# A hybrid decoder layer on one core: the order of the weight loads in the ten-set phase, and the tile of the fourth input sum

## The chip, the cores and the metric

The kernel runs on one core of one Trainium2 chip. The core has a matrix engine (PE), a vector engine (DVE), a scalar engine (ACT), a general-purpose engine (POOL) and a synchronisation engine (SP). SP, ACT and POOL can issue DMA transfers between the chip's memory (HBM) and the core's on-chip memory; the profile shows the issues of SP in queue q1 and those of POOL in queue q0. The metric is the device time of one execution in microseconds; the time of a kernel is the median of its runs.

## What is computed

One layer of a decoder trunk for 256 tokens of width 2048: an RMSNorm, one wide input projection, two token mixers side by side (gated linear attention and differential attention), two branch projections, a gated merge, an output projection, a second RMSNorm and the residual. Cut to what matters here:

```python
h = rmsnorm(x, pre_norm_g[l])
proj = h @ w_in[l]
(a_q, a_k, a_v, a_g, a_lr, b_q, b_k, b_v, b_g, m_a, m_b) = jnp.split(proj, offsets, axis=-1)
gk = jax.nn.log_sigmoid(a_lr @ gla_gk_w2[l] + gla_gk_b[l]) / GATE_LOGIT_NORMALIZER
o_a = rmsnorm(gla_chunked(a_q, a_k, a_v, gk), gla_norm_g[l]) * jax.nn.silu(a_g)
o_b = rmsnorm(diff_attention(b_q, b_k, b_v, lam), diff_norm_g[l]) * (1.0 - lam_init)
o_b = o_b * jax.nn.silu(b_g)
merged = jax.nn.sigmoid(m_a) * (o_a @ w_branch_a[l]) + jax.nn.sigmoid(m_b) * (o_b @ w_branch_b[l])
x = x + rmsnorm(merged @ w_out[l], post_norm_g[l])
```

The weights and the inputs are float32. The change touches the stage that computes ten blocks of 1024 columns of `proj` (a_g, b_v, b_g, m_a and m_b).

## The kernel before

**Halves.** All weights pass through PE in pieces of 128 x 1024 values, called halves, in one fixed sequence (`seq`). For each half ACT rounds it to a high part (`hi`, line 355), DVE subtracts to get the low part (`lo`, line 356), and PE multiplies with both (line 563): six matmuls of 512 columns for a half of a set. `take` hands PE the next half; it calls `emit_half` so that three halves (`AHEAD`) are written into the program ahead of the one in use. `hi` and `lo` have three buffers each.

**Sets.** The ten sets are computed with seven products in place of eight block products (Strassen's way): the 2048 rows and the 1024 columns are cut into two by two blocks, and `PRODUCTS = (1, 3, 2, 5, 6, 7, 4)` is the order in which `block_products` takes them. Each product has two tiles (t = 0, 1) of two halves (h = 0, 1), so a set has 28 halves. Their weights are:

- `a`, two tiles of 128 x 2048: the first row block. It is the operand of product 1. Then the second block is added to it in memory by DMA, and later DVE adds to it on the chip, so that products 5, 6 and 4 read changed values.
- `b`, two tiles: the fourth block. It is the operand of product 3; during products 5 and 6 DVE adds `b` to `a`, then the second block is added to `b` by DMA, and product 7 reads it.
- `c`, four tiles of 128 x 1024: the third block, the operand of product 2, added to `a` during product 7.

The first load of `a` or `b` is a "link" (`link`, line 223: 1 MB, from SP for set 0, from POOL for the others), and the additions by DMA are line 248 (0.5 MB each, POOL). `a` and `b` come from a pool of six tiles, tag `chain`. `c` comes from the pool `big`, tag `u`, which has 18 tiles for everything of this size: the split input `xs` (eight tiles through the whole phase), the raw input `xraw` (four), gate halves `gr` and `gl`, parts of q and k, and more. `c` is loaded by SP (line 240).

**Partners.** Between the halves of a set stand halves of other matrices (`v4`, `k..`, `q..`, then `dq..`, `dk..`), two in a tile called `raw` with three buffers (line 306, SP). A set of the steady part has three such tiles, their halves behind products 2, 5, 6 and 7; set 0 has four more halves.

**Order.** The framework orders the instructions of each engine itself, by their place in the program and by when their inputs and tiles are ready in its own model. `tc.keep_in_program_order` pins an instruction behind the one of the same engine that stands before it in the program. In the set phase the matmuls, the links, the additions by DMA and the spills are pinned. The loads of `c` and of `raw` are not, so a load may go out ahead of one that stands before it in the program. All DMAs of POOL stand in one line, and an instruction that waits holds up those behind it; the same goes for SP.

**Where the links and spills stand.** Before, the links of the next set are written at products 6 (`a`) and 7 and 4 (`b`). The gate halves `gr` and `gl` of a set are spilled to memory by POOL at `SPILL_AT` in the next set, that is at product 5; a `u` tile is free when its spill has landed.

**Input sums.** Products 3, 5, 6 and 7 multiply with sums of input blocks (`s4`, `r1`, `s2`, `r3`), made by `sum_operands` before the phase, but for the fourth, `r3`: `last_sum` (lines 741 to 745) is written into the phase after six steps (`PUT_OFF`) and takes a `u` tile of its own. The other three are made in two tiles of the `chain` pool, `temps`; each has two halves, and the second half of `temps[1]` is not used:

```python
r1, s2, s4 = (temps[n // 2][:, n % 2] for n in range(3))
```

`last_sum` is the last reader of `xraw[0]` and `xraw[1]`.

**The loads in `emit_half`.** A raw tile's load is written into the program when its first half is the next to be emitted:

```python
while loaded[0] < min(j + 2, len(seq)):
    if len(seq[loaded[0]]) == 3 and seq[loaded[0]][2] == 0:
        load(loaded[0])
    loaded[0] += 1
```

Of the kernel before, what the change touches and what calls it, by code (L numbers as in the profile page):

```python
# [14 lines left out]
P = 128  # L15
# [15 lines left out]
MERGE = (0, 1, 6, 7)  # L31
GLA_GATES = (8, 9)
LEAD = 11
PAIRS = [(g, pair) for g in range(4) for pair in range(2)]
EARLY = 3
PARTNERED = ((2, 1), (5, 1), (6, 0), (6, 1), (7, 0), (7, 1))
MORE_PARTNERS = ((0, 1, 0), (0, 1, 1), (0, 3, 1), (0, 5, 0))
SPILL_AT = (5, 0, 0)
PACE = {"linear": 1.5, "pairs": 1.75}
BIG = 18  # L40
MORE = 16
# [58 lines left out]
def phase_steps():  # L100

    keys = ["v4"] + [f"{name}{hf}{c}" for hf in range(2) for name in ("k", "q") for c in range(4)]
    keys += [f"{name}{g}{c}" for g, pair in PAIRS[:EARLY] for name in ("dq", "dk") for c in (2 * pair, 2 * pair + 1)]
    other = [(key, r, h) for key in keys for r in range(4 if key == "v4" else 1) for h in range(2)]
    slots = [(s, prod, t) for s in range(SETS) for prod in PRODUCTS for t in range(2)]
    mixed = []
    for slot in slots:
        mixed += [("set", *slot, h) for h in range(2)]
        s, prod, t = slot
        for _ in range(((prod, t) in PARTNERED) + (slot in MORE_PARTNERS)):  # L110
            mixed.append(other.pop(0))
    return mixed + other
# [11 lines left out]
def branch_steps():  # L124

    plain = [("y03", r, h) for r in (2, 3) for h in range(2)]
    plain += [(f"y1{g}", r, h) for g in range(2) for r in range(2) for h in range(2)]
    parts = half_set_steps("ys0")
    return [(plain, parts)[n == "p"].pop(0) for n in BRANCH_ORDER]


def late_steps():

    plain = [(f"y1{g}", r, h) for g in (2, 3) for r in range(4) for h in range(2)]
    plain += [(f"o{g}", r, h) for r in range(2) for g in range(2) for h in range(2)]
    parts = half_set_steps("os0") + half_set_steps("os1")
    return [(plain, parts)[n == "p"].pop(0) for n in LATE_ORDER]
# [3 lines left out]
def hybrid_kernel(ctx: ExitStack, tc, xt, xn, preg, postg, w, w2, gkb, glag, lamv, diffg, ident_d, causal_d, lmask_d, out):  # L141
    nc = tc.nc
    pe, act, dve, pool, sp = nc.tensor, nc.scalar, nc.vector, nc.gpsimd, nc.sync
# [12 lines left out]
    def u(shape, name, dtype=F32):  # L156
        count[0] += 1
        return big.tile(shape, dtype, tag="u", name=f"{name}_{count[0]}")
# [28 lines left out]
    def f32(ap):  # L187
        return ap.bitcast(F32)
# [10 lines left out]
    def halves_of(*keys):  # L199
        return [(key, r, h) for key in keys for r in range(len(at[key])) for h in range(2)]  # L200

    def heads_order(pairs):
        return halves_of(*(f"{name}{g}{c}" for g, pair in pairs for name in ("dq", "dk") for c in (2 * pair, 2 * pair + 1)))

    seq = halves_of("v0", "v2", "v3") + phase_steps()
    seq += heads_order(PAIRS[EARLY:]) + halves_of(*(f"y0{g}" for g in range(4)))[:-4]
    seq += branch_steps() + late_steps() + halves_of("o2", "o3")
    ready = {}
    emitted = [0]
    raws = {}  # L210
    chain = {}

    def weights(key, r):
        a, size = at[key][r]
        return w[a : a + P * size].rearrange("(p n) -> p n", p=P), size

    def block(s, i, t):
        return weights(f"set{s}", 2 * i + t)[0]
# [8 lines left out]

    def emit_set(s, prod, t, h):
        c = slice(1024 * h, 1024 * h + 1024)
        name, i = {(6, 0): ("a", 0), (6, 1): ("a", 1), (7, 1): ("b", 0), (4, 0): ("b", 1)}.get((prod, t), (None, 0))  # L230
        if h == 0 and name and s + 1 < SETS:
            link(s + 1, name, i)
        if h == 0 and s == 0 and prod == 1:
            link(s, "b", t)
        for ahead in range(min(2, SETS - s)):
            n = 4 * (PRODUCTS.index(prod) - PRODUCTS.index(2)) + 2 * t + h - 28 * ahead + (LEAD if s + ahead else 6)
            if 0 <= n < 4:
                i, j = n // 2, n % 2
                raws[s + ahead, i, j] = u([P, 1024], "c")
                sp.dma_start(raws[s + ahead, i, j], block(s + ahead, 2, i)[:, 1024 * j : 1024 * j + 1024])  # L240
        a, b = chain[s, "a", t], chain[s, "b", t]
        return raws[s, t, h] if prod == 2 else (b if prod in (3, 7) else a)[:, c]

# [50 lines left out]
    def load(j):  # L294
        key, r, h = seq[j]
        src, size = weights(key, r)
        n = size // 2
        early = key == "v0"
        if key == "v3" and r == 0:
            for i in range(2):  # L300
                link(0, "a", i)
        count[0] += 1
        raw = raws[key, r] = wpool.tile([P, 2048], F32, tag="raw", name=f"raw_{count[0]}")
        cuts = (0, n, size) if j in (0, 2) else (0, size)
        for a, b in zip(cuts, cuts[1:]):
            i = sp.dma_start(raw[:, a:b], src[:, a:b])
            if early or key[0] == "o" or key in ("y10", "y11", "y12", "y13", "ys0"):
                tc.keep_in_program_order(i)
        if early and j // 2 in X_LOADS:
            load_x(*X_LOADS[j // 2])  # L310

    def emit_plain(j, key, r, h):
        n = at[key][r][1] // 2
        if key == "v0":
            if j:
                prep_x(j)
            if 6 <= j < 14:
                square_x(j - 6)
        return raws[key, r][:, n * h : n * h + n]

    loaded = [0]

    def emit_half():
        j = emitted[0]
# [77 lines left out]
    def square_x(i):  # L402
        src = xraw[i // 2][:, 2 * (i % 2) : 2 * (i % 2) + 2, :].rearrange("p a t -> p (a t)")
        t = t2([P, 512], "xsq") if i else ssum
        tc.keep_in_program_order(act.activation(t, src, AF.Square))
        if i:
            dve.tensor_tensor(out=ssum, in0=ssum, in1=t, op=ALU.add)
# [96 lines left out]
    done = set()  # L504
# [55 lines left out]
    pinned = [False]  # L560
# [144 lines left out]
    def sum_operands():  # L705
        for kt in range(KT):
            x = xraw[kt // 4][:, kt % 4, :]
            act.activation(x, x, AF.Copy, scale=preg_s[:, kt : kt + 1])
            if kt % 4 == 3:
                yield  # L710
        temps = []
        for n in range(2):
            count[0] += 1
            temps.append(blocks.tile([P, 2, 8, P], F32, tag="chain", name=f"temp_{count[0]}", bufs=6))
        r1, s2, s4 = (temps[n // 2][:, n % 2] for n in range(3))

        def part(i, j, q):
            return xraw[2 * j + q][:, :, P * i : P * i + P]

        def rows(t, q):  # L720
            return t[:, 4 * q : 4 * q + 4]

        def split(name, t):
            hi, lo = (blocks.tile([P, 8, P], F32R, tag=f"{name}{e}", name=f"{name}{e}", bufs=1) for e in "hl")
            act.activation(hi, t, AF.Copy)
            dve.tensor_tensor(out=lo, in0=t, in1=f32(hi), op=ALU.subtract)
            sums[name] = hi, lo

        for q in range(2):
            dve.tensor_tensor(out=rows(r1, q), in0=part(1, 1, q), in1=part(1, 0, q), op=ALU.subtract)  # L730
            dve.scalar_tensor_tensor(out=rows(s2, q), in0=rows(r1, q), scalar=-1.0, in1=part(0, 0, q), op0=ALU.mult, op1=ALU.subtract)
        yield
        for q in range(2):
            dve.scalar_tensor_tensor(out=rows(s4, q), in0=rows(s2, q), scalar=-1.0, in1=part(0, 1, q), op0=ALU.mult, op1=ALU.subtract)
        split("s4", s4)
        yield
        split("r1", r1)
        yield
        split("s2", s2)

        def last_sum():
            r3 = u([P, 8, P], "r3")
            for q in range(2):
                dve.tensor_tensor(out=rows(r3, q), in0=part(0, 0, q), in1=part(1, 0, q), op=ALU.subtract)
            split("r3", r3)

        put_off.append(last_sum)

    def late():
# [32 lines left out]
    def others():  # L782
# [7 lines left out]
        for hf in range(2):  # L790
            for name in ("k", "q"):
                part = u([P, 2, 4, P], name)
                for c in range(4):
                    o = ps("bg")
                    for h in range(2):
# [10 lines left out]
                        yield  # L806
        for g, pair in PAIRS[:EARLY]:
            for name in ("dq", "dk"):
# [24 lines left out]
    def block_products(s):  # L833
# [20 lines left out]
        for prod in PRODUCTS:  # L854
# [3 lines left out]
            for t in range(2):  # L858
                for h in range(2):
                    if (prod, t, h) == SPILL_AT:  # L860
                        settle_owed()
# [41 lines left out]

    sets = (step for s in range(SETS) for step in block_products(s))
    rest = others()
    pinned[0] = True
    fetched = []
    for n, step in enumerate(phase_steps()):
        if n == PUT_OFF:
# [3 lines left out]
        next(sets if step[0] == "set" else rest)  # L913
    for gen in (sets, rest):
        assert next(gen, DONE) is DONE
    pinned[0] = False
    joint.close()
    more = ctx.enter_context(tc.tile_pool(name="more", bufs=MORE))
    pools[:] = ctx.enter_context(tc.tile_pool(name="small", bufs=2)), more
# [377 lines left out]
    m0 = gspill[12:16]  # L1297
    for g, pair in PAIRS[EARLY:]:
        diff_heads(g, pair)
# [251 lines left out]
    for g in (2, 3):  # L1551
# [7 lines left out]
        if g == 2:  # L1559
            total(0, 2, bank, 2)  # L1560
            for b in range(2):
                xres.append([])
                for i in range(2):
                    t = u([P, 1024], "xres")
# [3 lines left out]
    t = total(0, 3, bank)  # L1568
# [10 lines left out]
    for c in range(2):  # L1579
# [6 lines left out]
        if c == 0:  # L1586
            t = cell(1, 3)[:, :256]
# [4 lines left out]
        else:  # L1592
            end = ps("bg")
            c = slice(TURNED[0] % 1024, TURNED[0] % 1024 + 512)
            t = yg[1, 1][:, c]
# [67 lines left out]
```

## Time and profile before

| | |
|---|---|
| median of 3 runs | 1094.99 us (1094.82 to 1095.22) |
| the profiled execution | 1098.81 us |
| its span, first to last instruction | 1097.0 us |
| mean granted TensorE clock | 0.993 |
| matmuls | 5380 |
| DVE, ACT busy | 88%, 69% of the span |
| moved by DMA | 295.55 MB, mean 269 GB/s |
| DMA queues, share of 16 engines | q1 (SP) 42.8%, q0 (POOL) 42.3% |

The profile shows one execution. Busy time of PE overstates its work, since matmuls overlap and their ends are modelled; where PE waits is better read from the starts of its matmuls in the chain of work that ended last. A row of the timeline gives start, length, engine, line, operation, output<-inputs, and in brackets the idle time of the engine just before it and what ended it. Tiles go by their names in the program without numbers: `mm` and `bg` are accumulation banks, `in_w_dram` the packed weights. "DMA to landing" counts from the issuing instruction's start to the arrival of the last byte. The phase of the ten sets runs from about 84 to 652 us of the span.

### The profile page before, as it was taken

The page shows a single profiled execution, that of the slowest core. Times are in us where ns is not written, and L with a number is a line of the kernel's source. Part 1 is how long each engine was busy: PE and PEld are TensorE (multiplying, and loading weights), DVE is VectorE, ACT ScalarE, POOL GpSimd, SP SyncE. Part 2 cuts the span into 40 slices and gives each one's busy share as a digit, 9 for nine tenths or more (in the row PEclk, how much of TensorE's full clock was granted, in tenths as well). Part 3 has the DMA queues.
Part 4 walks back from the last instruction along what each step waited for, and adds up shares of the span by engine and source line. Part 5 has one row for each costly group of instructions (what it writes and reads, how often), then busy time and mean ns, then how long its engine had stood idle before and what let it go on. Part 6 is the DMA issues. An engine that isn't in the chain of part 4 may idle for free.

```text
span 1097.0 us, 15424 instructions
## 1 busy us (share of the span) xinstructions
PE 1075.8 (98%) x5380; PEld 917.7 (84%) x5380; DVE 963.6 (88%) x1289; ACT 758.1 (69%) x1090; POOL 177.3 (16%) x259
## 2 busy tenths in 40 slices
PE   9999899999999999999999999999999999999997
PEld 8998788888878888878788888898987888888886
DVE  7887989999999999989899998985877878889896
ACT  7886676777676767667676776665766777566662
POOL 0211212121212121221121212013110112100000
PEclk9999999999999999999999999999999999999999
DMA  9898987989797979797979778759988998989752
GB/s 354 284 324 242 291 254 209 343 215 327 208 338 205 353 205 351 200 329 191 350 167 373 173 250 307 230 201 333 310 299 257 282 312 266 338 292 259 268 187 101
DMA packets 68366, 295.55 MB, mean 269 GB/s; under 512 B 8832, under 2 KB 11904, under 8 KB 51648
## 3 DMA queue, kind: packets, MB, share of 16 engines
q1 hardware_dynamic: 38080, 167.99, 42.8%
q0 software_dynamic: 29632, 125.84, 42.3%
q8 instruction: 42, 0.69, 0.3%
q10 hardware_dynamic: 576, 0.73, 0.2%
q14 instruction: 36, 0.29, 0.1%
HBM read 267.27 MB, written 27.26 MB: 268 GB/s over the span
## 4 chain that ended last, share of the span: by engine, by line
PE 82%; DVE 6%; DMA 5%; issue 4%; ACT 2%; POOL 1%; POOLq 0%; ACTq 0%; DVEq 0%
PE mm L563 56%; PE bg L563 17%; DMA b<-in_w_dram 3%; DVE lo L356 2%; PE mm L551 2%; PE bg L551 2%; PE mm L536 1%; PE bg L997 1%; DMA dh<-dh 1%; PE bg L536 1%; DVE a L256 1%; ACT hi L355 1%; ACT prob L1142 1%; DMA c<-in_w_dram 1%; DVE prob L1136 1%
## 5 line engine op out<-in xcount | busy, mean ns | idle before, releaser
L355 ACT ACTIVATE hi<-raw 128x1024 fp32r<-128x1024 f32 (+3 forms) x213 | 217.7, 1026 | 122.5 <-PE mm L563 68.1
L356 DVE TENSOR_TENSOR lo<-raw,hi 128x1024 fp32r<-128x1024 f32 (+3 forms) x215 | 252.6, 1180 | 34.0 <-ACT hi L355 31.8
L355 ACT ACTIVATE hi<-a 128x1024 fp32r<-128x1024 f32 x160 | 168.8, 1060 | 47.8 <-PE mm L563 30.9
L356 DVE TENSOR_TENSOR lo<-a,hi 128x1024 fp32r<-128x1024 f32 x160 | 190.1, 1219 | 6.1 <-ACT hi L355 4.6
L563 PE MATMUL mm<-hi,xs 128*128 128x512 f32 (+1 forms) x608 | 155.9, 382 | 1.4 <-ACT hi L355 1.4
L563 PEld LDWEIGHTS mm<-hi,xs 128*128 128x128 f32 x608 | 113.9, 188 | 20.4 <-ACT hi L355 1.8
L563 PE MATMUL bg<-xs,hi 128*128 128x512 f32 x448 | 117.8, 396 | 0.0
L355 ACT ACTIVATE hi<-b 128x1024 fp32r<-128x1024 f32 x80 | 84.6, 1060 | 40.2 <-DMA b<-in_w_dram 19.1
L356 DVE TENSOR_TENSOR lo<-b,hi 128x1024 fp32r<-128x1024 f32 x80 | 97.9, 1223 | 15.6 <-ACT hi L355 13.0
L563 PEld LDWEIGHTS bg<-xs,hi 128*128 128x128 f32 x448 | 86.2, 192 | 17.3
L563 PE MATMUL mm<-lo,xs 128*128 128x512 f32 (+1 forms) x304 | 88.6, 381 | 0.1
L563 PE MATMUL mm<-xs,hi 128*128 128x512 f32 x320 | 82.2, 394 | 0.0
L248 POOL DMA_DIRECT2D b<-in_w_dram x40 | 35.0, 875 | 210.1 <-DVE a L256 78.4
L563 PEld LDWEIGHTS bg<-xs,lo 128*128 128x128 f32 x448 | 60.9, 190 | 6.3 <-DVE lo L356 2.1
L563 PEld LDWEIGHTS mm<-xs,hi 128*128 128x128 f32 x320 | 57.4, 189 | 10.0
L563 PEld LDWEIGHTS mm<-lo,xs 128*128 128x128 f32 x304 | 56.8, 188 | 10.1 <-DVE lo L356 0.5
L563 PE MATMUL bg<-xs,lo 128*128 128x256 f32 x448 | 62.9, 283 | 0.7 <-DVE lo L356 0.7
L356 DVE TENSOR_TENSOR lo<-c,hi 128x1024 fp32r<-128x1024 f32 x40 | 49.0, 1226 | 9.1 <-ACT hi L355 5.0
L355 ACT ACTIVATE hi<-c 128x1024 fp32r<-128x1024 f32 x40 | 42.5, 1063 | 15.3 <-PE mm L563 10.5
L563 PE MATMUL mm<-hi,oah 128*128 128x512 f32 x128 | 50.6, 396 | 0.5 <-DVE part L1309 0.5
L563 PE MATMUL mm<-hi,oal 128*128 128x512 f32 x128 | 50.1, 391 | 0.0
L256 DVE TENSOR_TENSOR a<-a,b 128x1024 f32<-128x1024 f32 x40 | 48.9, 1222 | 0.7
(407 smaller groups left out, 2280.5 us busy)
## 6 DMA issues: line engine op xcount, KB each, us to landing
raw<-in_w_dram SPq DMA_DIRECT2D x90, 1024.0 KB, 7.9
c<-in_w_dram SPq DMA_DIRECT2D x40, 512.0 KB, 12.4
a<-in_w_dram POOLq DMA_DIRECT2D x40, 512.0 KB, 9.6
b<-in_w_dram POOLq DMA_DIRECT2D x40, 512.0 KB, 10.0
a<-in_w_dram POOLq DMA_DIRECT2D x18, 1024.0 KB, 14.6
b<-in_w_dram POOLq DMA_DIRECT2D x18, 1024.0 KB, 9.9
raw<-in_w_dram SPq DMA_DIRECT2D x14, 832.0 KB, 6.8
gr<-gr POOLq DMA_DIRECT2D x10, 512.0 KB, 6.2
```

The source lines that it names most:

```text
L248: tc.keep_in_program_order(pool.dma_start(chain[s, name, i][:, c], block(s, 1, i)[:, c], accum_op=ALU.add))
L256: add = dve.tensor_tensor(out=a, in0=a, in1=chain[s, "b", i][:, c] if second else raws[s, i, h], op=ALU.add)
L355: act.activation(hi_t[:, a:b], r[:, a:b], AF.Copy)
L356: dve.tensor_tensor(out=lo_t[:, a:b], in0=r[:, a:b], in1=f32(hi_t[:, a:b]), op=ALU.subtract)
L536: i = pe.matmul(out, lhs, rhs, start=first and n == 0, stop=last and n == len(pairs) - 1, **kw)
L551: i = pe.matmul(banks[g][b][:, :n], a[part][:, P * b : P * b + P], w[:, n * g : n * g + n], start=first, stop=last)
L563: i = pe.matmul(*args, **kw)
L997: pe.matmul(o, xk[:, P * c : P * c + P], xq.rearrange("p (b c t) -> p b c t", b=2, c=4)[:, :, c, :], start=i == 0, stop=i == 1)
L1136: dve.tensor_tensor_reduce(out=prob[m][:, lo:up], in0=banks[b][:, n * m : n * m + n], in1=cm[:, lo:up], scale=1.0, scalar=-3e38, op0=ALU.a ...
L1142: act.activation(prob[m][:, lo:up], prob[m][:, lo:up], AF.Exp, scale=score_scale[:, b : b + 1], bias=mx[:, i : i + 1], accum_out=z[:, i : ...
```

## The change

Four things are changed, and no arithmetic. First, the links of `a` for the next set are written at product 3 (second tile) and product 2 (first tile) in place of product 6; those of `b` stay. Second, the gate halves of the set before are spilled at product 3 in place of product 5. Third, within the phase the loads of `c` and of `raw` are pinned to program order, and at three places of each set (`RAWS_AT`) the next raw tile that isn't loaded yet is loaded early, as long as fewer than three are in use by the program's count (`alive`). Fourth, `r3` is computed in the unused half of `temps[1]`.

```diff
+LINKS = {(3, 1): ("a", 0), (2, 0): ("a", 1), (7, 1): ("b", 0), (4, 0): ("b", 1)}
+RAWS_AT = ((4, 1, 0), (2, 0, 1), (5, 1, 0))
-SPILL_AT = (5, 0, 0)
+SPILL_AT = (3, 0, 0)
...
     def emit_set(s, prod, t, h):
-        name, i = {(6, 0): ("a", 0), (6, 1): ("a", 1), (7, 1): ("b", 0), (4, 0): ("b", 1)}.get((prod, t), (None, 0))
+        name, i = LINKS.get((prod, t), (None, 0))
...
-                sp.dma_start(raws[s + ahead, i, j], block(s + ahead, 2, i)[:, 1024 * j : 1024 * j + 1024])
+                tc.keep_in_program_order(sp.dma_start(raws[s + ahead, i, j], block(s + ahead, 2, i)[:, 1024 * j : 1024 * j + 1024]))
+        if (prod, t, h) in RAWS_AT:
+            load_next(emitted[0])
...
     def load(j):
+        alive[0] += 1
-            if early or key[0] == "o" or key in ("y10", "y11", "y12", "y13", "ys0"):
+            if early or joint_loads[0] or key[0] == "o" or key in ("y10", "y11", "y12", "y13", "ys0"):
                 tc.keep_in_program_order(i)
...
     def emit_plain(j, key, r, h):
+        alive[0] -= h
...
+    def load_next(done):
+        j = max(loaded[0], done)
+        while j < len(seq) and not (len(seq[j]) == 3 and seq[j][2] == 0):
+            j += 1
+        if j < len(seq) and alive[0] < 3:
+            load(j)
+            loaded[0] = j + 1
...
         def last_sum():
-            r3 = u([P, 8, P], "r3")
+            r3 = temps[1][:, 1]
...
-    pinned[0] = True
+    pinned[0] = joint_loads[0] = True
...
-    pinned[0] = False
+    pinned[0] = joint_loads[0] = False
```

Written out for a set of the steady part, the program order of SP's loads becomes: the first two `c` of the next set, its first raw tile, the other two `c`, and then, within the next set, its second and third raw tile. In set 0 it is: four `c`, then the raw tiles of `v4` one after another.

More of the change, by code (lines that the diff above doesn't have):

```diff
@@ L318, in emit_plain @@
                 square_x(j - 6)
+        alive[0] -= h
         return raws[key, r][:, n * h : n * h + n]
     loaded = [0]
+    joint_loads = [False]
+    alive = [0]
+    def load_next(done):
[5 more added lines that the diff above has]
+            loaded[0] = j + 1
     def emit_half():
```

## The prediction

> **What bounds the kernel now.** I read the page's busy times first.
>
> ```profile
> PE 1075.8 (98%) x5380; PEld 917.7 (84%) x5380; DVE 963.6 (88%) x1289; ACT 758.1 (69%) x1090; POOL 177.3 (16%) x259
> ```
>
> PE carries the time, and the change leaves its matmuls alone. What can be won is PE's idle time between 84 us and 652 us, where the ten sets run. The chain in order of time gives it: columns are start, length, what.
>
> ```profile
> 84.47 2.18 PE bg L563 x12
> ...
> 144.18 2.77 PE bg L563 x16
> 146.95 21.78 PE mm L563 x96
> ...
> 201.79 21.78 PE mm L563 x96
> ...
> 651.71 26.71 PE mm L563 x144
> ```
>
> A row of 96 matmuls (16 halves: the last product of one set and the first three of the next) starts each period. 201.79 - 146.95 = 54.84 us is a period without a wait. Nine of them would take 493.6; from 146.95 to 651.71 there are 504.8. **Sets 1 to 9 lose 11.2 us.** The stretch from 84.47 to 146.95 holds 22 halves of set 0 (at 21.78/16 = 1.36), eight of `v4` (2.18) and two of `k00` (2.77): 52.9 us of work in 62.5, so **set 0 loses 9.6**. Together 20.8 us, which is all that this change can win.
>
> Next, windows (us, PE, PEld, DVE, ACT and POOL busy, granted clock, DMA share, GB/s) around the worst places, and the waits between 147 and 652 us (total, times, longest).
>
> ```profile
> 276.60:281.00 4.40, 4.40 (x24) 3.74 (x23) 4.23 (x4) 3.24 (x4) 0.06 (x1) 1.00 0.01 2
> 281.00:306.60 25.60, 25.60 (x131) 21.83 (x130) 24.62 (x25) 14.91 (x17) 6.77 (x10) 1.00 0.97 286
> 259.00:276.60 17.60, 17.60 (x79) 14.60 (x78) 16.24 (x16) 14.84 (x16) 3.50 (x4) 1.00 0.96 243
> ...
> 132.00:139.00 7.00, 6.41 (x15) 4.85 (x16) 7.00 (x8) 4.46 (x5) 1.08 (x2) 0.52 1.00 370
> 473.00:482.00 9.00, 6.68 (x26) 5.01 (x25) 8.12 (x8) 4.50 (x7) 2.22 (x4) 0.81 1.03 420
> 530.00:539.00 9.00, 6.83 (x25) 4.87 (x25) 6.17 (x7) 5.23 (x6) 0.54 (x1) 0.81 1.02 422
> ```
>
> ```profile
> ACT hi L355 <- DMA b<-in_w_dram: 19.1, 8, 3.3
> ...
> ACT dq L771 <- DMA dh<-dh: 5.1, 1, 5.1
> ```
>
> In nearly every set ACT waits some 2.4 us for the second row block that is added into a `b` tile. Mostly PE's lead hides it; in sets 6 and 7 it doesn't: PE is idle 2.3 and 2.2 us, and the clock of 0.81 over 9 us means 3.4 us at half speed, another 1.7 each. That is 7.9 of the 11.2. In set 7 the wait is for the spill `dh`, which stands in POOL's queue behind the same additions.
>
> **Part 1: the links of `a`.** POOL's DMA order in set 3, and from issue to landing the last addition into `b` in set 3 (issued at 291.30) and in set 9 (631.5), which has no next set and so no links:
>
> ```profile
> 283.95 0.85 POOL L223 DMA_DIRECT2D a<-in_w_dram  x1
> 287.89 0.89 POOL L248 DMA_DIRECT2D b<-in_w_dram  x1 [3.09 <-ACT hi L355]
> 291.30 0.88 POOL L248 DMA_DIRECT2D b<-in_w_dram  x1 [2.51 <-ACT q L800]
> ```
>
> ```profile
> DMA to landing us min/median/max: 15.2/15.2/15.2
> ```
>
> ```profile
> DMA to landing us min/median/max: 8.5/8.5/8.5
> ```
>
> A link of 1 MB stands between the additions into `b0` and `b1`, one more follows, and the two spills of the set before go out there too. The diff moves both links and both spills to products 3 and 2, behind the additions into `a` (issued 262.5 to 266.0). They cost POOL the same 0.85 and 0.56 us there, with nothing urgent behind them before 281. All six `chain` tiles stay enough: the slot that the link takes was `a` of the set before, last read in product 4. So the last addition lands about 8.5 instead of 15.2 us after 291.3, near 300 instead of 306.5. ACT waited some 2.4 us for it, so it is wanted near 304: the wait goes. `dh`, right behind it, lands by about the same 6 us sooner, which covers its 5.1. What is late next is nothing of the DMA: set 1 already runs at 54.84. I leave 0.7 us of the 11.2, so **-10.5**.
>
> Against this speaks room: three more MB go to the lighter stretch. The windows show a hole of 4.4 us (share 0.01) ahead of 25.6 us at 0.97. At 420 GB/s, as in the windows at 473 and 530, 3 MB take 7.1 us, so some 2.7 run on into the additions of `b`, which have 4 to spare.
>
> **Part 2: the fourth input sum.** DVE's timeline at the end of set 0:
>
> ```profile
> 127.06 1.22 DVE L256 TENSOR_TENSOR a<-a,c 128x1024 f32<-128x1024 f32 x1
> ...
> 129.33 1.29 DVE L744 TENSOR_TENSOR r<-xraw 128x512 f32<-128x512 f32 x2
> 130.53 0.68 DVE L890 TENSOR_TENSOR gl<-mm,p 128x512 f32<-128x512 f32 x1
> 131.13 0.68 DVE L885 TENSOR_TENSOR gr<-mm,p 128x512 f32<-128x512 f32 x1
> ```
>
> The sum waits for one of 18 `u` tiles, freed by the addition of `c` at 127.06; by reading `xraw[0]` and `[1]` it frees the two that `gl` and `gr` take next. PE waits for `gr` and `r3`, and the window from 132 shows it half-clocked. In the half of `temps[1]` that `s4` doesn't use, the sum needs no `u` tile: 1.3 us of subtractions and the split move to where DVE (88% busy) has gaps, earlier in set 0 or before it. Then two `u` tiles are free when `gl` and `gr` come: this wait, some 7 of the 9.6, goes. The price is that `temps[1]` is held longer, and the second link for set 1 waits for it on POOL; behind it stands nothing but the additions into `b`, which follow product 5, two products on. Cost zero.
>
> **Part 3: SP in program order.** SP's issues in set 0 with the middle one of the three raw tiles by itself, the landing of the four loads of `c`, and the conversions around them:
>
> ```profile
> 69.37 9.34 SPq L306 DMA_DIRECT2D raw<-in_w_dram  x3
> 78.75 17.59 SPq L240 DMA_DIRECT2D c<-in_w_dram  x4
> ```
>
> ```profile
> L306 SPq DMA_DIRECT2D raw<-in_w_dram x1: 328/328/328, 75.4 to 75.4; - x1
> ```
>
> ```profile
> DMA to landing us min/median/max: 7.4/8.4/12.6
> ```
>
> ```profile
> 93.95 0.88 ACT L355 ACTIVATE hi<-raw 128x800 fp32r<-128x800 f32 x1 [0.32 <-PE mm L563]
> ...
> 102.35 1.06 ACT L355 ACTIVATE hi<-c 128x1024 fp32r<-128x1024 f32 x1 [4.62 <-DMA c<-in_w_dram]
> ```
>
> The last two `c` wait for `u` tiles until about 95 (102.35 less the shortest landing, 7.4), which costs PE the remaining 2 us or so of set 0. With the `xraw` tiles freed early they follow the first two at once. But the second `v4` tile, now issued ahead of all four, has its line behind them in the program and is pinned there. Two raw tiles and two `c` (2.7 MB) took from 75.4 to 91.9 us (79.3 and the longest landing, 12.6), 0.163 MB/us. Four `c` and one raw tile (2.9 MB) from 78.75 land near 96.6, against a conversion due at 93.95. PE's lead covers some 2 us, as the hidden waits for `b` show, so PE loses about 0.6. The bounds: 0 if the tiles are free sooner; about 11 if the last two `c` still go at 95 and 96 and the raw tile behind them lands near 105 (9.4 idle and 1.7 at half clock). I take 1.5, with what the moved sum displaces, near the end where the tiles are free: the sum's inputs are those of the three sums that are made before set 0. So **-8.1** in set 0.
>
> In the later sets the order becomes `c`, `c`, raw, `c`, `c`, raw, raw. Raw tiles now go out as soon as one of three buffers is free, a set early:
>
> ```profile
> 286.24 10.64 SPq L306 DMA_DIRECT2D raw<-in_w_dram  x2
> 307.83 1.75 SPq L240 DMA_DIRECT2D c<-in_w_dram  x4
> ```
>
> The first would go behind two `c`, by these rows near 309, 23 us later, and is needed 16 halves (21.8 us) on. So 1 MB more leaves the window of the additions into `b`. The three early-load calls issue no further DMA. Nothing is priced, and the bound upward is rival C.
>
> **Sum.** 20.8 - 0.7 - 1.5 = 18.6 us. The profiled execution took 1098.81 (span 1097.0 and 1.81 around it), so it would take 1080.2. The median of the three runs is 3.82 below the profiled one: 1076.4 if those runs hold the same waits, up to 1080.2 if the 3.82 is waits that only the profiled one has. I take **1077.5**, nearer to the first, since the second needs all of it to be such waits.
>
> **Rivals.**
>
> *A, the wait moves to `a`.* [...] The additions into `a` and the conversions of product 5:
>
> ```profile
> DMA to landing us min/median/max: 6.2/8.9/10.6
> ```
>
> ```profile
> 282.34 1.06 ACT L355 ACTIVATE hi<-a 128x1024 fp32r<-128x1024 f32 x1 [0.82 <-PE mm L563]
> ```
>
> The last one, issued at 266.0, lands at 276.6 and is needed at 282.3; with PE's 2 us of lead it may take 18 us instead of 10.6 before PE stalls. The links stand behind it in the queue, so it should not; if they mix in wholly, 7.1 us and later raw tiles reach that point. A stall as in set 6, 4.0 us in each of nine sets, is +36 against the 18.6 gained: **1112, slower**.
>
> *B, set 0 is blocked on SP.* The upper bound of part 3: 11 + 0.5 stay instead of 1.5, **1087.5**.
>
> *C, new waits for `u` tiles, or `b` still late.* If two `c` of the next set take the tiles that `gr` needs, PE waits for product 7's first addition, by the timings of set 3 under 0.5 to 1 us a set; if one raw or `c` load keeps `b` late, about half of the 11.2 stays. Either leaves 5 to 9: **1084**. The landing of 8.5 in set 9 speaks against.
>
> *D, it does nothing measurable*, with set 0's gain eaten by B and the sets' by C together: **1094**.
>
> **How the numbers follow.** Forecast (1074 to 1081) 0.58; B 0.15; C 0.14; D 0.05; A 0.08. The low end is 1074.0, nearly all of the 20.8 gone; 1089 takes in B and C and leaves out A, D and the forecast's edges. This kernel's runs can tell 0.2%, 2.2 us. Faster 0.87, same 0.05, slower 0.08.
>
> **What would show it.** Right: ACT's waits for `b` near zero and additions into `b` landing within 9 us; the fourth sum ahead of 95 us and no half clock at 132, 477 and 535; every period 54.8 to 55. Wrong: a wait of ACT for `raw` near 94 to 105 (B), for `a` in product 5 (A), or PE waiting for `gr` each set (C).

## The result, and the profile after

The changed kernel takes **1081.05 us** (median of four runs, 1080.91 to 1081.12); the kernel before takes 1095.11 beside it (1094.82 to 1097.38). The ratio is 0.9867 with a 95% interval of 0.9850 to 0.9884. The forecast was 1077.5, its range 1074.0 to 1089.0. The measured time is 3.55 above the forecast; it lies in the range, but a hair outside the 1074 to 1081 that the prediction gave to its own case. The profiled execution of the changed kernel took 1081.1, as much as its other runs.

First the busy times on the page of the changed kernel:

```profile
PE 1066.9 (99%) x5380; PEld 914.4 (85%) x5380; DVE 961.8 (89%) x1289; ACT 759.2 (70%) x1090; POOL 177.8 (16%) x259
```

Its chain of work in order of time (start, length, what):

```profile
138.98 21.78 PE mm L579 x96
...
193.82 21.78 PE mm L579 x96
...
413.18 21.78 PE mm L579 x96
...
468.62 21.78 PE mm L579 x96
...
523.46 21.78 PE mm L579 x96
...
579.22 21.78 PE mm L579 x96
...
634.06 26.72 PE mm L579 x144
```

Read it as before: the first row ends set 0, the distance from row to row is a period. Set 0 ends at 138.98 instead of 146.95. From there to 634.06 are 495.08 us, where nine periods of 54.84 make 493.6: sets 1 to 9 lose 1.5 instead of 11.2. Only 413.18 to 468.62 (set 6, 55.44) and 523.46 to 579.22 (set 8, 55.76) are longer than 54.84, and miss the sign of 54.8 to 55 that the prediction named. From 634.06 to the end of the span (1079.3) are 445.2, and 445.3 before. So all of the difference lies in the ten sets: 8.0 in set 0 and 9.7 in the others.

POOL's DMA order in set 3 of the changed kernel (start, length, what, and the idle time before it with its releaser), and the landing of the last addition into `b`:

```profile
257.85 0.85 POOL L252 DMA_DIRECT2D a<-in_w_dram  x1 [0.66 <-DVE lo L372]
258.39 0.86 POOL L225 DMA_DIRECT2D a<-in_w_dram  x1
258.95 0.86 POOL L177 DMA_DIRECT2D gr<-gr  x1
259.49 0.84 POOL L177 DMA_DIRECT2D gl<-gl  x1
260.02 0.83 POOL L225 DMA_DIRECT2D a<-in_w_dram  x1
272.80 0.90 POOL L252 DMA_DIRECT2D b<-in_w_dram  x1 [11.95 <-DVE a L260]
...
283.12 0.85 POOL L252 DMA_DIRECT2D b<-in_w_dram  x1 [2.54 <-ACT q L816]
```

```profile
DMA to landing us min/median/max: 5.9/5.9/5.9
```

Links and spills go out together behind the additions into `a`, nothing stands between the additions into `b`, and the last of these lands 5.9 us after its issue instead of 15.2. From 84 to 652 us, the waits of the changed kernel (total, times, longest) hold none for the DMA of `b` or `c` any more, and for that of `dh` 0.2 us:

```profile
PE bg L579 <- DVE lo L372: 1.5, 3, 0.7
...
ACT dq L787 <- DMA dh<-dh: 0.2, 1, 0.2
```

The fourth input sum stands far ahead of 95 us on DVE's timeline, and windows of the changed kernel at the end of set 0 and over the other sets show the full clock (1.00):

```profile
63.33 1.29 DVE L760 TENSOR_TENSOR temp<-xraw 128x512 f32<-128x512 f32 x2
```

```profile
130.00:140.00 10.00, 9.29 (x48) 7.33 (x47) 9.75 (x11) 5.05 (x7) 1.64 (x3) 1.00 1.00 338
...
139.00:634.00 495.00, 494.00 (x2377) 416.36 (x2377) 473.62 (x451) 362.88 (x393) 100.28 (x140) 1.00 0.92 277
```

### The profile page after: what moved, and what is told of

The parts are those of the page before. It is cut to its first block, busy times and chain, and to the rows that moved or that the text cites. A ratio compares the mean times of both kernels' runs of the same rounds, so it can differ in the third digit from the quotient of the medians.

```text
span 1079.3 us, 15427 instructions
## 1 busy us (share of the span) xinstructions
PE 1066.9 (99%) x5380; PEld 914.4 (85%) x5380; DVE 961.8 (89%) x1289; ACT 759.2 (70%) x1090; POOL 177.8 (16%) x259
## 4 chain that ended last, share of the span: by engine, by line
PE 88%; DVE 6%; issue 3%; ACT 1%; POOL 1%; DMA 0%; POOLq 0%; SPq 0%; DVEq 0%; ACTq 0%
PE mm L579 59%; PE bg L579 20%; DVE lo L372 2%; PE mm L567 2%; PE bg L567 2%; PE mm L552 1%; PE bg L1013 1%; DVE a L260 1%; PE bg L552 1%; ACT prob L1158 1%; DVE prob L1152 1%; POOL de L474 0%; DMA raw<-in_w_dram 0%; PE bg L1172 0%; PE bg L1064 0%
## 5 line engine op out<-in xcount | busy, mean ns | idle before, releaser
L579 PEld LDWEIGHTS mm<-hi,xs 128*128 128x128 f32 x608 | 114.0, 188 | 18.6
L579 PE MATMUL bg<-xs,hi 128*128 128x512 f32 x448 | 115.4, 390 | 0.0
L579 PEld LDWEIGHTS bg<-xs,hi 128*128 128x128 f32 x448 | 84.2, 188 | 16.4
L371 ACT ACTIVATE hi<-b 128x1024 fp32r<-128x1024 f32 x80 | 84.1, 1059 | 19.2 <-PE mm L579 17.3
L371 ACT ACTIVATE hi<-c 128x1024 fp32r<-128x1024 f32 x40 | 42.5, 1063 | 12.0 <-PE mm L579 11.2
```

The source lines that it names most:

```text
L371: act.activation(hi_t[:, a:b], r[:, a:b], AF.Copy)
L579: i = pe.matmul(*args, **kw)
```

## The experiments

All kernels were timed beside the kernel before. The short table has the medians, the end of set 0, and the time from there to the last row of the ten sets, all from the chain of each profile:

| kernel | us, median | set 0 ends | sets 1 to 9 |
|---|---|---|---|
| before, profile of the prediction | 1094.99 | 146.95 | 504.76 |
| before, profiled again | 1095.47 | 144.06 | 503.48 |
| links only | 1091.75 | 149.24 | 495.09 |
| sum only | 1088.96 | 138.66 | 504.06 |
| SP's order and sum | 1085.72 | 138.87 | 499.32 |
| links and sum | 1080.93 | 138.60 | 495.09 |
| spills and sum | 1080.84 | 138.58 | 495.09 |
| all but SP's order | 1080.84 | 138.76 | 495.08 |
| all but the sum | 1099.69 | 155.44 | 495.08 |
| the whole change | 1081.05 | 138.98 | 495.08 |

### The kernel before, profiled a second time

No edit.

> The kernel before, unchanged, profiled a second time. Theory: the 3.8 us by which its first profiled execution (1098.81) is above the median of its timed runs are waits that not every execution has, in sets 6 and 7: this profile's sets 1 to 9 then lose 7 to 9 us instead of 11.2, set 0 still 9.6, and the execution takes 1095 to 1097. Rival: a profiled execution of this kernel always takes about 3.8 us more than a timed one: 1098.5 to 1099.1 again, with 2.2 us waits and half a clock at 474 and 531.

Measured: 1095.47 (1093.33 to 1099.63 in ten runs); the profiled execution took 1094.66, with a span of 1092.9. So the profile doesn't always cost 3.8 us, and timed runs of this kernel spread over 6 us, where those of the changed one spread over 0.2. The waits differ from execution to execution, as the theory said, but not where it said. Sets 1 to 9 lost 9.9 us, more than the 7 to 9 expected; set 0 lost some 7.0 in place of 9.6 (from about 84.2 to 144.06 are 59.9, of which 52.9 are work), and 2.9 us of the 4.1 by which the spans differ lie ahead of the end of set 0. Part of the reason is the clock. A row of PE's timeline and a window (columns as in the prediction) of the first profile, then the same of the second:

```profile
131.96 0.47 PE L563 MATMUL mm<-hi,r3h 128*128 128x512 f32 x1 [3.16 <-DVE gr L885]
```

```profile
132.00:147.00 15.00, 14.41 (x57) 11.71 (x58) 12.87 (x13) 8.37 (x9) 1.62 (x3) 0.77 0.96 341
```

```profile
130.30 0.47 PE L563 MATMUL mm<-hi,r3h 128*128 128x512 f32 x1 [3.16 <-DVE gr L885]
```

```profile
130.00:144.00 14.00, 13.12 (x57) 10.80 (x58) 13.01 (x14) 8.69 (x10) 1.63 (x3) 0.88 0.98 348
```

The same wait of 3.16 us was followed by 6.9 us at half clock in one (0.23 of 15 us, doubled) and by 3.4 in the other (0.12 of 14, doubled).

### Only the links of `a`

Against the kernel before:

```diff
+LINKS = {(3, 1): ("a", 0), (2, 0): ("a", 1), (7, 1): ("b", 0), (4, 0): ("b", 1)}
...
-        name, i = {(6, 0): ("a", 0), (6, 1): ("a", 1), (7, 1): ("b", 0), (4, 0): ("b", 1)}.get((prod, t), (None, 0))
+        name, i = LINKS.get((prod, t), (None, 0))
```

> Only the two links of `a` move, to products 3 and 2; spills, fourth sum and SP's loads as before. Theory: the links alone keep the last addition into `b` late; it lands 9 us or less after its issue, ACT's waits for `b` fall below 3 us in all, sets 1 to 9 lose under 2 us, set 0 its 9.6: 1087 to 1089. Rival: the raw tiles that SP sends meanwhile keep `b` late as well, and the addition lands some 12 us after its issue: 1091 to 1094.

Measured: 1091.75, ratio 0.9975 (0.9962 to 0.9988). The time is in the rival's range, but not for the rival's reason. In the sets the theory holds: 1.5 us lost, no wait for `b`, though the last addition into `b` of set 3 landed 10.0 us after its issue and not within 9. But set 0 got longer. Its rows, POOL's and then ACT's:

```profile
87.82 1.43 POOL L225 DMA_DIRECT2D a<-in_w_dram  x2
```

```profile
103.06 1.06 ACT L371 ACTIVATE hi<-c 128x1024 fp32r<-128x1024 f32 x1 [4.99 <-DMA c<-in_w_dram]
106.78 1.06 ACT L371 ACTIVATE hi<-c 128x1024 fp32r<-128x1024 f32 x1 [2.66 <-DMA c<-in_w_dram]
```

The last two loads of `c` still go out near 95 us, since they wait for `u` tiles, and now find 2 MB of links on the way that were issued at 87.82. ACT waits 7.65 us for them instead of 4.8. Without the sum the links take back in set 0 part of what they win later: its end is 2.3 us later than in the first profile of before, and 5.2 later than in the second.

### Only the fourth input sum

Against the kernel before:

```diff
-            r3 = u([P, 8, P], "r3")
+            r3 = temps[1][:, 1]
```

> Only the fourth input sum goes into the unused half of the temporary; links, spills and SP's loads as before. Theory: the wait at 128 to 139 goes and with it the half clock there; set 0 loses 1 to 2.5 us instead of 9.6: 1086 to 1088.5. Rival: without an order on SP the loads of `c` or the tile of `v4` behind them come late in its place, and set 0 keeps 5 us or more: 1090 to 1094.

Measured: 1088.96, ratio 0.9945 (0.9929 to 0.9961). Set 0 ends at 138.66 and loses 1.7 us (its first row of `v4` starts at 84.08, and 52.9 are work), as the theory has it, with no order on SP: the loads of `c` aren't late in its place. Sets 1 to 9 still lose 10.5, with 19.2 us of waits for `b`, and the median is 0.5 us above what was expected (1086 to 1088.5). One of their stalls bears on the clock as well. First the kernel before, then this one:

```profile
476.76 0.97 PE L563 MATMUL mm<-lo,r3h 128*128 128x512 f32 x2 [2.32 <-DVE lo L356]
```

```profile
468.06 0.73 PE L579 MATMUL mm<-lo,r3h 128*128 128x512 f32 x2 [2.32 <-DVE lo L372]
```

```profile
464.00:474.00 10.00, 7.13 (x33) 5.17 (x32) 8.59 (x9) 6.26 (x9) 2.22 (x4) 1.00 1.03 422
```

The same stall of 2.32 us: at 476.76 half a clock followed (0.81 over 9 us, in the prediction's windows), at 468.06 none (1.00).

### All but the order on SP

Against the changed kernel:

```diff
-RAWS_AT = ((4, 1, 0), (2, 0, 1), (5, 1, 0))
+RAWS_AT = ()
...
-                tc.keep_in_program_order(sp.dma_start(raws[s + ahead, i, j], block(s + ahead, 2, i)[:, 1024 * j : 1024 * j + 1024]))
+                sp.dma_start(raws[s + ahead, i, j], block(s + ahead, 2, i)[:, 1024 * j : 1024 * j + 1024])
...
-            if early or joint_loads[0] or key[0] == "o" or key in ("y10", "y11", "y12", "y13", "ys0"):
+            if early or key[0] == "o" or key in ("y10", "y11", "y12", "y13", "ys0"):
```

> The changed kernel without its part on SP: loads of `c` and raw tiles with no pin and no early calls; links, spills and the sum as changed. Theory: the part on SP is worth little: sets 1 to 9 lose under 3 us, set 0 under 3: 1081 to 1083.5. Rival: the raw tiles a set early push the additions into `b` back, or set 0 has its `c` late: 1085 to 1090.

Measured: 1080.84 (1080.53 to 1081.06), ratio 0.9870 (0.9856 to 0.9885). It is the time of the whole change, just below what was expected (1081 to 1083.5): beside the other parts, the order on SP is worth nothing.

### All but the sum

Against the changed kernel:

```diff
-            r3 = temps[1][:, 1]
+            r3 = u([P, 8, P], "r3")
```

> The changed kernel, but the fourth input sum is kept in a `u` tile again; links, spills and the order on SP as changed. Theory (the mechanism of rival B): the last two loads of `c` in set 0 wait for `u` tiles until about 95 us and the second `v4` tile, now pinned behind them, lands near 105 instead of 86; ACT waits for it 8 to 11 us, set 0 loses 18 or more: 1097 to 1104, slower than before. Rival: the tile isn't held up, and only set 0's old waits return: 1090 to 1093, as with the links alone (1091.75).

Measured: **1099.69**, ratio 1.0044 (1.0029 to 1.0059): slower than before. SP's issues in set 0, then ACT's wait and PE's:

```profile
75.80 16.25 SPq L242 DMA_DIRECT2D c<-in_w_dram  x4
92.10 1.77 SPq L311 DMA_DIRECT2D raw<-in_w_dram  x3
```

```profile
106.06 0.87 ACT L371 ACTIVATE hi<-raw 128x800 fp32r<-128x800 f32 x1 [13.15 <-DMA raw<-in_w_dram]
```

```profile
106.99 0.70 PE L579 MATMUL bg<-hi,xs 128*128 128x400 f32 x1 [10.61 <-ACT hi L371]
```

This is rival B, alive as soon as the `u` tiles are short: the four loads of `c` take until 92 to get out, ACT waits 13.15 us for the raw tile that is pinned behind them, and PE stands for 10.61 us. The changed kernel shows the other case:

```profile
69.66 9.32 SPq L242 DMA_DIRECT2D c<-in_w_dram  x4
79.08 9.11 SPq L311 DMA_DIRECT2D raw<-in_w_dram  x3
```

All four are out before 79, and the raw tile issued at 79.08 lands 7.2 us later, 7.6 ahead of the 93.95 at which it was due before. Sets 1 to 9 lose 1.5 here too. So parts 2 and 3 aren't independent: the order on SP needs the free tile.

### Links and sum, with the spills left; spills and sum, with the links left

The first has `SPILL_AT = (5, 0, 0)` and the new `LINKS`, the second `SPILL_AT = (3, 0, 0)` and the old `LINKS`. Both keep the sum in `temps[1]` and have no order on SP.

> Links of `a` and fourth input sum moved, spills of `gr` and `gl` at product 5 as before, SP as before. Theory: the links were what kept `b` late, and the spills cost nothing measurable where they stood: 1080.5 to 1082 (links, spills and sum together took 1080.84). Rival: 1 MB of spills ahead of the additions into `b` keeps them some 2 to 3 us late, with waits in sets 6 and 7: 1083 to 1087.

> Spills and fourth input sum moved, links of `a` at product 6 as before, SP as before. Theory: with the links between and behind the additions into `b`, these stay late, and the spills change nothing: 1087.5 to 1089.5 (the sum alone took 1088.96). Rival: the spills are half of the gain of part 1: 1083.5 to 1086.

Measured: 1080.93, ratio 0.9872 (0.9857 to 0.9887), and 1080.84, ratio 0.9871 (0.9856 to 0.9886). The first came as the theory had it. In the second both theory and rival fell: with the links where they always were, between and behind the additions into `b`, moving 1 MB of spills is enough. The last addition into `b` of set 3, issued at 282.8 in the sum alone and at 282.7 in these two; one answer of each, in this order:

```profile
DMA to landing us min/median/max: 15.0/15.0/15.0
```

```profile
DMA to landing us min/median/max: 10.7/10.7/10.7
```

```profile
DMA to landing us min/median/max: 10.2/10.2/10.2
```

Either move takes some 4.5 us off, and that is more than the wait of about 2.4. Both moves together bring the landing down to 6.8 (all but SP's order; 5.9 with it) and the time nowhere, since PE waits for it no longer. The links weren't the cause by themselves; by these runs the stretch was overfull by a little, whatever stood in it.

### The order on SP and the sum, links and spills left

The old `LINKS` and `SPILL_AT = (5, 0, 0)` in the changed kernel.

> Order on SP and fourth input sum as changed, links of `a` and spills of `gr` and `gl` where they were. After the runs in which either the links or the spills alone were enough. Theory: the window of the additions into `b` is overfull by a little; taking any one load out of it is enough, the raw tile that SP's order sends later too: last addition into `b` some 10 us after its issue, 1080.5 to 1082. Rival: raw tiles on another queue don't count against POOL's additions; they stay at 14 us and the waits in sets 6 and 7 stay: 1086 to 1089, as with the sum alone (1088.96).

Measured: 1085.72, ratio 0.9908 (0.9879 to 0.9937), between the two ranges expected. One answer for the same addition, and the waits that are left from 147 to 652 us:

```profile
DMA to landing us min/median/max: 9.5/9.5/9.5
```

```profile
ACT dq L787 <- DMA dh<-dh: 4.4, 1, 4.4
...
ACT hi L371 <- DMA b<-in_w_dram: 2.6, 2, 1.5
```

With the sum alone, SP issues two raw tiles, of 1 MB each, at 277.76 and 288.07, around the addition at 282.8; here SP issues nothing from 247 to 293.8. So in this kernel raw tiles on SP's queue count against POOL's additions: 15.0 becomes 9.5, the waits for `b` fall from 19.2 to 2.6, and sets 1 to 9 lose 5.8 instead of 10.5. What stays is the wait for `dh` behind the additions in set 7. So the prediction was wrong to price this part at nothing in the later sets by itself (it is worth 4.7 us between the two profiles, and 3.2 between the medians, 1088.96 and 1085.72), and right for it beside part 1 (zero).

### What the changed kernel still loses: a partner moved

Its remaining 3.2 us lie at the ends of sets 0, 6 and 8, counted by the rows of the chain; the expectations below call the last two 5 and 7. DVE and then PE at the end of set 6 of the changed kernel:

```profile
464.16 1.21 DVE L260 TENSOR_TENSOR a<-a,c 128x1024 f32<-128x1024 f32 x1
465.29 0.69 DVE L910 TENSOR_TENSOR gr<-mm,p 128x512 f32<-128x512 f32 x1
465.89 1.22 DVE L372 TENSOR_TENSOR lo<-raw,hi 128x1024 fp32r<-128x1024 f32 x1
```

```profile
467.17 1.22 PE L579 MATMUL bg<-xs,lo 128*128 128x256 f32 x8 [0.33 <-DVE lo L372]
```

DVE works without a gap, and PE waits for the low half of the partner (`lo<-raw`). It looked as if one partner less at the set's end would do. Three kernels moved one of the six to the end of product 3, the first the one of `(7, 1)`, the others that of `(7, 0)` and `(6, 0)`:

```diff
-PARTNERED = ((2, 1), (5, 1), (6, 0), (6, 1), (7, 0), (7, 1))
+PARTNERED = ((3, 1), (2, 1), (5, 1), (6, 0), (6, 1), (7, 0))
```

> The changed kernel with one of the six partner halves of each set moved from the end of product 7 to the end of product 3. Theory: what PE still loses, 3.2 us, comes from DVE crowded at the end of sets 0, 5 and 7, and with one partner's conversions less there half or more of it goes: 1078.5 to 1080. Rival: its raw tile then falls on the full stretch of DMA ahead of product 5, or tiles come late in other places: 1081 to 1086.

> The changed kernel with the partner half of product 7's first row block, not the second, moved to the end of product 3. Theory: the half between product 7 and product 4 covers the read of the shared bank by `gr` (PE lost 1.0 to 1.8 us a set when it was taken away), and stays here; DVE has one partner less to convert ahead of it, and the losses at the ends of sets 0, 5 and 7 go: 1078 to 1080. Rival: conversions and buffers come late in another place: 1081 to 1086.

> The changed kernel with the partner half of product 6's first row block moved to the end of product 3. Theory: like the run with product 7's, with DVE eased further from the set's end: 1078.5 to 1080.5. Rival: 1081 to 1086, with a new wait of PE.

Measured: 1098.06, 1100.25 and 1091.04 (ratios 1.0026, 1.0045 and 0.9959): all slower than the changed kernel, by 17, 19 and 10 us, and outside what theory and rival gave. PE's waits from 84 to 652 us in the three:

```profile
PE mm L579 <- DVE gr L910: 12.1, 10, 1.6
```

```profile
PE mm L579 <- DVE lo L372: 7.9, 16, 0.6
...
PE bg L579 <- DVE lo L372: 5.3, 10, 0.6
```

```profile
PE bg L579 <- DVE lo L372: 4.8, 10, 0.5
```

In the first, product 4 follows product 7 at once and has to wait in every set until `gr` has read the bank that they share. In the other two, PE waits for conversions in every set. These waits (12.1, 13.2 and 4.8 us) are only part of the 17, 19 and 10; the rest was not followed. The reading seems to have been the wrong way round, as the groups of DVE from 282 to 304 us of the changed kernel show (count, busy us and mean ns of one, then idle time):

```profile
L372 DVE TENSOR_TENSOR lo<-raw,hi 128x1024 fp32r<-128x1024 f32 x4 | 4.9, 1217 | 0.2 <-ACT hi L371 0.2
L372 DVE TENSOR_TENSOR lo<-b,hi 128x1024 fp32r<-128x1024 f32 x4 | 4.9, 1217 | 0.7 <-ACT hi L371 0.7
L260 DVE TENSOR_TENSOR a<-a,c 128x1024 f32<-128x1024 f32 x4 | 4.9, 1216 | 0.0
```

A half of product 7 costs DVE a conversion and an addition, 2.43 us, while PE works on it for 1.36. A partner half costs DVE 1.22 and a few small operations, and gives PE 2.77. By these times partners are where DVE catches up, not what crowds it. So the last kernel went the other way and moved the partner of `(2, 1)` to `(7, 0)`, which then has two:

```diff
-PARTNERED = ((2, 1), (5, 1), (6, 0), (6, 1), (7, 0), (7, 1))
+PARTNERED = ((5, 1), (6, 0), (6, 1), (7, 0), (7, 0), (7, 1))
...
-        for _ in range(((prod, t) in PARTNERED) + (slot in MORE_PARTNERS)):
+        for _ in range(PARTNERED.count((prod, t)) + (slot in MORE_PARTNERS)):
```

> The changed kernel with the partner half of product 2 moved the other way, to product 7, whose first row block then has two. Theory, from the three runs with a partner taken out of products 6 and 7 (each lost more there): a partner half gives PE 2.77 us of work for 1.6 to 1.9 us of DVE's, while a half of product 7 gives 1.36 for 2.4, so partners are what lets DVE catch up; with one more of them the losses at the ends of sets 0, 5 and 7 go: 1078 to 1080. Rival: product 5 comes 2.77 us earlier and meets additions into `a` or `b`, or raw tiles, that aren't there yet, or the second partner's tile is late: 1081.5 to 1088.

Measured: 1082.10 (1081.75 to 1082.91), ratio 0.9882 (0.9862 to 0.9901): no gain, and if anything 1 us more. Its chain, where a period runs from one row to the next:

```profile
358.97 27.22 PE mm L579 x120
...
413.98 27.22 PE mm L579 x120
...
469.00 27.22 PE mm L579 x120
...
524.39 27.22 PE mm L579 x120
...
579.41 27.22 PE mm L579 x120
```

The period that took 55.44 now takes 55.02 (413.98 to 469.00), and the one of 55.76 takes 55.02 too. But the undisturbed ones went from 54.84 to 55.01 (358.97 to 413.98), and the one from 469.00 to 55.39. Half of the theory held, that a partner relieves the set's end; the other half, that nothing else would be late, didn't. What is left seems to go with DVE, which has little room in a set, as a window over most of set 3 of the changed kernel shows (PE, PEld, then DVE with 47.55 of 50 us); that it is the limit is argued, not shown. No version here clearly beats the changed kernel.

```profile
254.00:304.00 50.00, 50.00 (x244) 42.31 (x243) 47.55 (x45) 35.64 (x39) 10.85 (x15) 1.00 0.92 257
```

## Why the prediction was right, and where it was off

- **What bounds it.** Right: all of the difference lies in PE's idle time, and the half clock after it, between 84 and 652 us, and nothing behind it moved.
- **Part 1, -10.5.** Measured -9.7: 1.5 us stay instead of 0.7, and they are DVE's, not the DMA's. `b` landed earlier than forecast (5.9 after issue, 8.5 forecast). The stated mechanism, a late `b` because too much goes out beside it, holds. But the part is larger than it has to be: with the sum, moving either the links or the spills alone gives the whole.
- **Part 2, the larger part of set 0.** Right, and shown alone: the sum by itself brings the end of set 0 to 138.66. The cover named for the second link held: nothing waited behind it.
- **Part 3, 1.5 left in set 0.** 1.7 are left, but not for the reason given. The raw tile wasn't late (0 instead of 0.6); PE waits for DVE at the end of the set. The choice of the near end was right, because the tiles were free; the far end, 11, is what the kernel without the sum shows (PE stood for 10.61). The forecast that the first raw tile of a later set goes near 309 was wrong: in the changed kernel SP issues it at 292.47, directly behind two loads of `c` as said. Of these 16.5 us, 8.2 are only that set 3 starts earlier (248.66 in place of 256.83); for the rest, the loads of `c` go out earlier within the set, at 290.35.
- **The sum.** 18.6 forecast, 17.7 measured between the two profiled executions (1098.81 and 1081.1).
- **The step that was mis-sized** is the last: how the median of before stands to its profiled execution. I took the 3.82 us to be mostly no waits of that one execution, and put 1077.5 nearer to 1076.4 than to 1080.2. The second profile of before took 1094.66 and timed runs went up to 1099.63, with other waits and another share of half clock. In the second profile the ten sets lose some 16.9 us (7.0 and 9.9) in place of 20.8, and that is nearly all of the 4.15 by which it is faster. So the profiled execution was a slow one by its waits, the other end, 1080.2, was the one to take, and with the 0.9 by which the sum was too large it gives the 1081.1 that was measured. Both errors went the same way, and it was the wide range, made for rivals B and C, that took in the result.
- **The rivals.** B needs the sum to be left out; A didn't appear (ACT waits for no `a` in the changed kernel); of C, no new waits for `u` tiles came. D fell.

## What to carry over

Here a stretch of transfers ended some 2 us too late: taking the links or the spills out of it was enough (the last addition into `b` of set 3 landed 10.7 or 10.2 us after its issue instead of 15.0), and transfers on another queue counted too (sending SP's raw tiles later made it 9.5 and brought about half of the gain in sets 1 to 9: 5.8 us lost instead of 10.5). Test the parts alone before calling one the cause, since each of two moves gave the whole (1080.93 and 1080.84) and both together nothing more (1080.84). Before fixing an order on a queue, ask whether everything ahead in it can go out, and free the buffers first: the same order cost nothing with a free tile (1081.05 against 1080.84) and made the kernel slower than before without it (1099.69, with ACT waiting 13.15 us for the tile behind). And take gains from waits against the profiled execution in which they were measured, then ask whether that execution is typical, by profiling the kernel before a second time if the runs spread.

## What the runs showed of the hardware

The penalty after a stall of PE wasn't the same each time. After the same 3.16 us of idle, 6.9 us went at half clock in one execution of the kernel before and 3.4 in the next; after the same 2.32 us, 3.4 in the kernel before and none in the one with only the sum moved. Half clock is 0.50 as granted: windows of 1 us in the first profile of before show it in each from 133 to 139. So one stretch of 3.4 us at half clock costs 1.7 us, by an estimate from these two numbers. The runs of before spread over 6 us (1093.33 to 1099.63), while the changed kernel, without such stalls, stays within 0.2 (1080.91 to 1081.12). Half clock can be only a part of that: among the ten runs of before that go with its second profile, those with the same mean clock of 0.994 took 1094.66, 1097.72 and 1099.63, so most of the spread has another source, and the waits that differ between the two profiles are the likeliest one. What decides how long half clock lasts after a stall, or whether it follows at all, was not shown: no run here shifted a stall by itself to test that.
